# RWKV branch of an encoder layer: the group norm in three parts tied behind chunks, value shifts and loads tied behind later work, the norm's squares on VectorE

## The chip, the cores and the metric

The kernel runs on one core of a Trainium2 chip. The metric is device microseconds of one execution, the median of several runs on the same chip. Before the change it was 2368.71 us (three runs: 2364.8, 2368.71 and 2369.3).

Engine names in the rows: PE is TensorE (PEld its weight loads), DVE VectorE, ACT ScalarE, POOL GpSimd, SP SyncE. SP and POOL here mostly issue DMAs; each issues its own in the order of its instructions.

## The reference

One layer on 256 tokens of width 2048 in float32: a feed-forward block, two mixers in parallel (latent attention and RWKV-7) joined by gates, a cross-attention, a second feed-forward block. The change lies in the RWKV mixer:

```python
def rwkv7_branch(proj, mu_shift, w0, w_w2, a0, w_a2, w_g2, k_k, k_a, r_k, lnx_w, lnx_b, w_ob):
    p = token_shift(proj, mu_shift)              # y + (y_prev - y) * mu
    r, k, v, dw, da, dg = jnp.split(p, [...], axis=-1)
    g = jax.nn.sigmoid(dg) @ w_g2
    ...
    def step(state, inp):
        r_t, w_t, k_t, v_t, a_t, b_t = inp
        sa = jnp.einsum('bhvk,bhk->bhv', state, a_t)
        state = (state * w_t[:, :, None, :] + sa[..., None] * b_t[:, :, None, :]
                 + v_t[..., None] * k_t[:, :, None, :])
        return state, jnp.einsum('bhvk,bhk->bhv', state, r_t)
    _, o = lax.scan(step, s0, xs)                # 256 steps, 16 heads of 64
    ...
    mean = jnp.mean(o, axis=-1, keepdims=True)   # group norm, per head
    var = jnp.mean(jnp.square(o - mean), axis=-1, keepdims=True)
    o = ((o - mean) * lax.rsqrt(var + LNX_EPS)).reshape(B, S, C)
    o = o * lnx_w.astype(jnp.float32) + lnx_b.astype(jnp.float32)
    bonus = jnp.sum(rh * kh * r_k.astype(jnp.float32), axis=-1, keepdims=True) * vh
    return (((o + bonus.reshape(B, S, C)).astype(proj.dtype)) * g) @ w_ob
```

## The kernel before, in words

**The weight stream.** Every large product multiplies by weights that stream from memory. `weights` (line 192) loads tiles of 128x1024 floats on the SP queue (L203, four buffers `wraw`), and splits each into two parts that TensorE can take: ScalarE writes the high part `whi` (L205), VectorE the rest `wlo` (L206). The split tiles stand in a ring of three. One tile feeds 12 matmuls of 512 columns where the block is 512 wide (`lin_tok_steps`, L254 to L256: hi, lo, hi for each of two row halves), and a slot is freed when its last matmul is done. So each tile needs one turn of ScalarE and one of VectorE, and whatever else stands in these two queues delays the splits: an engine takes its instructions strictly in their written order.

**The mixer.** `mix` (line 1071) runs in stages. `rw_proj_v` (L715) projects the values in two blocks of 512 columns. Each half of a block is written to memory (`vraw`, L733), read back one row later (`vp`, L734), combined with a factor on VectorE (L735 to L737) and stored as `vsh` (L738). Then come the latent attention and, in one weave, the recurrent part together with a stream of plain products (`fill`: output products and eight gate blocks). `weave` writes TensorE's order by hand: a generator of recurrent steps yields how many microseconds of fill work should follow it.

**The recurrent part.** `rw_prep` (L748) makes decay, keys and receptances for each of two head groups; it loads two small weights `ww` on POOL (L754, L755), which the lora matmuls (L765) read. `rw_inverse` (L885) inverts small triangular blocks on VectorE, writes them to memory (`td`) and reads them back into `G` (L913). `rw_chain` (L926) then takes the 256 tokens in 8 chunks of 32. A chunk is: `po` + state (L954), `rhs` copy, `pu` (L964), `uv` copied half by ScalarE and half by VectorE (L967), `pn` (L973), the new state `S` on VectorE (L980, L981), `po` (L983), the next chunk's `po` (L939), `o` copied out (L991) and stored to `osc` on POOL (L993). Between those steps stand 9 to 12 matmuls of a gate block. `pn` waits for both halves of `uv`, so VectorE's copy is in the loop.

**Scale and norm.** For each half `t` of 128 tokens (four chunks) and each half `h` of the heads, `rw_scale` (L1000) loads `lnx_w`, `lnx_b` and the shifted values on POOL and prepares two factors `ab` (L1011 to L1017, with one matmul `pg` each, L1015). `rw_group_norm` (L1021) loads `ov` from `osc` on POOL and normalises: sum `gm` (L1029, L1030), subtraction (L1031), square on ScalarE (L1032), sum `gv` (L1033, L1034), the power -1/2 on POOL (L1035), and three products and sums (L1036 to L1038). The result is transposed (L334) into `z` for the last product. In `mix` the pieces for `t` = 0 are written as soon as two, four and six chunks have been stored, those for `t` = 1 behind the last chunk. They get a low priority, and a scheduler that plans with its own costs sets where each falls in an engine's queue. `after(a, b)` forces an order: a plain order if both are on one engine, a wait otherwise.

Of the kernel before, what the change touches and what calls it, by code (L numbers as in the profile page):

```python
# [10 lines left out]
F32 = mybir.dt.float32  # L11
F32R = mybir.dt.float32r
I32 = mybir.dt.int32
AF = mybir.ActivationFunctionType
# [4 lines left out]
P = 128  # L19
# [61 lines left out]
class Layer:  # L81
# [492 lines left out]
    def mla_heads(self, pool):  # L574
# [6 lines left out]
        for c in range(4):  # L581
# [132 lines left out]

    def rw_proj_v(self, mp, pool, normed):  # L715
        h, r, _ = normed
        nc = self.nc
        self.vraw = self.dram.tile([T + 1, 1024], F32, name="vraw")
# [5 lines left out]
        for c in range(2):  # L724
# [4 lines left out]
            def ev(t, ps):  # L729
# [19 lines left out]
    def rw_prep(self, pool, g, bon, ready):  # L749
# [5 lines left out]
        nc.gpsimd.dma_start(out=ww[64:], in_=a["w_a2"][:, cs])  # L755
# [243 lines left out]
    def rw_scale(self, pool, t, h, bon, behind):  # L999

        nc, a = self.nc, self.a
# [8 lines left out]
        v = ab[:, 1, :].rearrange("p (h v) -> p h v", v=64)  # L1010
        scaled = nc.vector.tensor_mul(v, v, bon[:, t, h * H : (h + 1) * H].unsqueeze(2).broadcast_to([P, H, 64]))  # L1011
        self.after(scaled, self.last_S)
        nc.vector.tensor_add(ab[:, 1, :], ab[:, 1, :], rows[:, 1, :])
        pg = self.psm.tile([P, 512], F32, tag="mm", name="pg")
        nc.tensor.matmul(pg, self.sg[:, ts], self.wg2[:, cs], start=True, stop=True)  # L1015
        self.after(nc.vector.tensor_mul(ab[:, 0, :], rows[:, 0, :], pg), self.last_S)
        nc.vector.tensor_mul(ab[:, 1, :], ab[:, 1, :], pg)  # L1017
        return ab

    def rw_group_norm(self, pool, t, h, ab):  # L1020
        nc = self.nc  # L1021
        H = HEADS_G
        ov = pool.tile([P, 2, 512], F32, tag="p4", name="ov", bufs=6)
        nc.gpsimd.dma_start(out=ov[:, 0, :], in_=self.osc[t * P : (t + 1) * P, h * 512 : (h + 1) * 512])
        o, sq = (ov[:, j, :].rearrange("p (h v) -> p h v", v=64) for j in range(2))
        bc = lambda x: x.unsqueeze(2).broadcast_to([P, H, 64])
        mean = self.stat.tile([P, H], F32, tag="gm", name="gm")
        var = self.stat.tile([P, H], F32, tag="gv", name="gv")
        nc.vector.tensor_reduce(out=mean, in_=o, axis=AX.X, op=ALU.add)  # L1029
        nc.vector.tensor_scalar_mul(mean, mean, 1.0 / 64)  # L1030
        nc.vector.tensor_sub(o, o, bc(mean))  # L1031
        nc.scalar.activation(out=sq, in_=o, func=AF.Square)  # L1032
        nc.vector.tensor_reduce(out=var, in_=sq, axis=AX.X, op=ALU.add)  # L1033
        nc.vector.tensor_scalar(out=var, in0=var, scalar1=1.0 / 64, scalar2=LNX_EPS, op0=ALU.mult, op1=ALU.add)  # L1034
        nc.gpsimd.tensor_tensor(out=var, in0=var, in1=self.mhalf.broadcast_to([P, H]), op=ALU.pow)  # L1035
        nc.vector.tensor_mul(o, o, bc(var))  # L1036
        nc.vector.tensor_mul(ov[:, 0, :], ov[:, 0, :], ab[:, 0, :])
        nc.vector.tensor_add(ov[:, 0, :], ov[:, 0, :], ab[:, 1, :])  # L1038
# [342 lines left out]
```

## Time and profile before

| | us |
|---|---|
| median of three runs | 2368.71 |
| lowest, highest | 2364.8, 2369.3 |
| the profiled execution, its own time | 2374.34 |
| its span, first to last instruction | 2372.2 |
| TensorE busy in the span | 2326.5 |
| mean granted TensorE clock, share of full | 0.991 |

TensorE is busy 98% of the span, so what can be gained without less work is in the 46 us in which it stood still, and in the stretches in which its clock was granted at half (1.2 instead of 2.4 GHz). Both are found stretch by stretch: a list of what TensorE waited for, and the granted clock by windows.

### The profile page before, as it was taken

Reading aid. Unit: us, or ns where it says so; the run is one execution under the profiler, and the core shown is the slowest. Engines: PE = TensorE matmul, PEld = TensorE weight load, DVE = VectorE, ACT = ScalarE, POOL = GpSimd, SP = SyncE. Lnnn points to the kernel's source line nnn. Section 1 sums busy time; section 2 is a strip of 40 time slices with the busy share of each in tenths; the row PEclk is TensorE's granted clock in tenths of the full one; section 3 lists DMA queues with packets and bytes.
Section 4 is the critical chain, followed back from the end, with each engine's and each line's share of the span. In section 5 each row is a group of like instructions: output and inputs, shape, how many; then the busy total and the mean of one; then the engine's idle time right before and its main releaser. Section 6 shows DMA issues by size and latency. Waiting matters only on the chain.

```text
span 2372.2 us, 34910 instructions
## 1 busy us (share of the span) xinstructions
PE 2326.5 (98%) x13610; PEld 1987.4 (84%) x13610; DVE 1453.2 (61%) x2117; ACT 1142.4 (48%) x1687; POOL 77.9 (3%) x128
## 2 busy tenths in 40 slices
PE   8999999999999999999999999999999999999997
PEld 7888888888887888888777788887888888888886
DVE  5666666654446576768556756656666666664444
ACT  6444544544446565534334546545544444444443
POOL 0000000000000100000122000000000000000000
PEclk9999999999999999999999999999999999999999
DMA  7555555566665664445647766545555555566664
GB/s 254 191 188 193 188 192 190 188 203 196 199 198 189 199 203 149 162 147 180 193 152 228 265 198 219 169 153 165 190 188 191 190 188 192 188 200 197 197 193 145
DMA packets 138821, 451.35 MB, mean 190 GB/s; under 512 B 24224, under 2 KB 26656, under 8 KB 138400
## 3 DMA queue, kind: packets, MB, share of 16 engines
q1 hardware_dynamic: 132992, 434.17, 56.4%
q0 software_dynamic: 4944, 14.69, 1.9%
q8 instruction: 106, 1.74, 0.3%
q10 hardware_dynamic: 720, 0.27, 0.1%
q14 instruction: 59, 0.48, 0.1%
HBM read 438.58 MB, written 10.49 MB: 189 GB/s over the span
## 4 chain that ended last, share of the span: by engine, by line
PE 49%; DVE 4%; DMA 2%; issue 1%; POOL 1%; ACT 0%; SPq 0%; DVEq 0%; POOLq 0%; ACTq 0%
PE mm L227 16%; PE mm L230 8%; PE mm L254 7%; PE mm L255 7%; PE mm L256 7%; DVE wlo L206 1%; DVE TT L908 0%; POOL gv L1035 0%; PE gr L870 0%; DVE X L436 0%; PE tr L361 0%; PE bt L874 0%; DVE tm L905 0%; PE xo L1260 0%; PE xsc L1249 0%
## 5 line engine op out<-in xcount | busy, mean ns | idle before, releaser
L206 DVE TENSOR_TENSOR wlo<-wraw,whi 128x1024 fp32r<-128x1024 f32 (+2 forms) x796 | 959.4, 1207 | 735.8 <-ACT whi L205 723.5
L205 ACT CAST whi<-wraw 128x1024 fp32r<-128x1024 f32 (+2 forms) x796 | 825.3, 1037 | 887.1 <-PE mm L256 453.5
L227 PE MATMUL mm<-hT,whi 128*128 128x512 f32 x3296 | 1149.5, 395 | 6.2 <-DVE hT L325 5.5
L230 PE MATMUL mm<-hT,wlo 128*128 128x256 f32 x3296 | 913.4, 283 | 2.0 <-DVE wlo L206 1.9
L227 PEld LDWEIGHTS mm<-hT,whi 128*128 128x128 f32 x3296 | 614.8, 189 | 134.8 <-ACT whi L205 6.3
L230 PEld LDWEIGHTS mm<-hT,wlo 128*128 128x128 f32 x3296 | 621.8, 189 | 12.5 <-DVE wlo L206 3.7
L254 PE MATMUL mm<-whi,mh 128*128 128x512 f32 x688 | 267.6, 389 | 0.0
L256 PE MATMUL mm<-whi,ml 128*128 128x512 f32 x688 | 267.6, 389 | 0.0
L255 PE MATMUL mm<-wlo,mh 128*128 128x512 f32 x688 | 267.6, 389 | 0.0
L255 PE MATMUL mm<-wlo,hT 128*128 128x512 f32 (+2 forms) x512 | 186.2, 364 | 6.7 <-DVE wlo L206 6.6
L254 PE MATMUL mm<-whi,hT 128*128 128x512 f32 (+2 forms) x512 | 190.4, 372 | 0.1
L256 PE MATMUL mm<-whi,hT 128*128 128x512 f32 (+2 forms) x512 | 185.0, 362 | 0.0
L254 PEld LDWEIGHTS mm<-whi,mh 128*128 128x128 f32 x688 | 129.1, 188 | 27.0
L256 PEld LDWEIGHTS mm<-whi,ml 128*128 128x128 f32 x688 | 129.1, 188 | 26.9
L255 PEld LDWEIGHTS mm<-wlo,mh 128*128 128x128 f32 x688 | 129.1, 188 | 26.6
L236 ACT COPY half<-mm 128x256 f32<-128x256 f32 x206 | 75.4, 367 | 135.2 <-PE mm L227 135.2
L237 DVE TENSOR_TENSOR half<-half,mm 128x256 f32<-128x256 f32 x206 | 86.0, 418 | 53.9 <-ACT half L236 53.9
L255 PEld LDWEIGHTS mm<-wlo,hT 128*128 128x128 f32 x512 | 97.5, 191 | 23.0 <-DVE wlo L206 9.8
L254 PEld LDWEIGHTS mm<-whi,hT 128*128 128x128 f32 x512 | 97.5, 190 | 16.4 <-ACT hT L324 0.5
L256 PEld LDWEIGHTS mm<-whi,hT 128*128 128x128 f32 x512 | 97.3, 190 | 14.4
L289 POOL TENSOR_TENSOR rstd<-rstd,mhalf 128x1 f32<-128x1 f32 x22 | 13.0, 597 | 1808.6 <-DVE rstd L287 1808.6
L254 PE MATMUL mm<-whi,oT 128*128 128x512 f32 x128 | 50.7, 396 | 0.0
(278 smaller groups left out, 1737.8 us busy)
## 6 DMA issues: line engine op xcount, KB each, us to landing
wraw<-in_w_ffn_up SPq DMA_DIRECT2D x172, 512.0 KB, 3.6
wraw<-in_w_ffn_gate SPq DMA_DIRECT2D x171, 512.0 KB, 4.2
wraw<-in_w_ffn_down SPq DMA_DIRECT2D x168, 512.0 KB, 4.2
wraw<-in_w_in SPq DMA_DIRECT2D x124, 512.0 KB, 3.5
wraw<-in_w_o SPq DMA_DIRECT2D x32, 512.0 KB, 3.5
wraw<-in_w_ckv SPq DMA_DIRECT2D x31, 512.0 KB, 3.5
wraw<-in_w_oa SPq DMA_DIRECT2D x16, 512.0 KB, 3.5
wraw<-in_w_ob SPq DMA_DIRECT2D x16, 512.0 KB, 4.3
```

Source lines behind the costliest of these rows:

```text
L205: cast = nc.scalar.copy(out=hi[:, e], in_=raw[:, e])
L206: self.last_split = nc.vector.tensor_sub(out=lo[:, e], in0=raw[:, e], in1=hi[:, e].bitcast(F32))
L227: both = lambda: nc.tensor.matmul(ps[j], hi[:, s], x[:, k], start=(k == 0), stop=(k == nk - 1))
L230: nc.tensor.matmul(ps[j][:, 0, :], lo[:, s], x[:, k, 0], start=False, stop=False)
L236: nc.scalar.copy(out=y, in_=ps[j][:, 1, :])
L237: nc.vector.tensor_add(y, y, ps[j][:, 0, :])
L254: nc.tensor.matmul(ps[t], part(xh, t, k), hi, start=(k == 0), stop=False)
L255: nc.tensor.matmul(ps[t], part(xh, t, k), lo, start=False, stop=False)
L256: self.last_mm = nc.tensor.matmul(ps[t], part(xl, t, k), hi, start=False, stop=(k == nk - 1))
L289: nc.gpsimd.tensor_tensor(out=r, in0=r, in1=self.mhalf, op=ALU.pow)
```

## The change

1. Value shift: the four VectorE instructions and the store of each half (L735 to L738) are put into a list, and written later: those of the first block in the middle of the second block's loop, those of the second block in `mla_heads`. The first instruction is tied behind the last split written by then.
2. The loads of `uv` for the first three chunks are tied behind the small `ww` loads.
3. `w_g2` and the `lnx`, `ab` loads of `t` = 0 were tied behind the write of the inverse; now they follow the store of the first chunk. Those of `t` = 1 follow the store of the seventh chunk (before, of the sixth). The arithmetic of `rw_scale` is separated: for `t` = 0 behind the third chunk, for `t` = 1 behind the last one.
4. The group norm takes both halves `h` together and has three parts: loads; sums up to the power; products. For `t` = 0 they are written behind the fourth, fifth and sixth chunk and tied behind that chunk's state update; the transposes follow the seventh. For `t` = 1 they are written behind the chain with 10 and 7 us of fill between, tied behind the last split.
5. The square is a VectorE product instead of a ScalarE activation.

```diff
+            if c == 1:
+                self.do_later()
...
-                nc.vector.tensor_sub(prev, prev, cur)
-                nc.vector.tensor_mul(prev, prev, mu)
-                nc.vector.tensor_add(prev, prev, cur)
-                nc.gpsimd.dma_start(out=self.vsh[t * P : (t + 1) * P, s], in_=prev)
-
-            self.lin_tok(self.a["w_in"], KD, 2880 + c * 512, 512, h[:, :, 0], h[:, :, 1], ev)
+
+                def shift(t=t, s=s, mu=mu):
+                    self.after(nc.vector.tensor_sub(prev, prev, cur), self.last_split)
+                    nc.vector.tensor_mul(prev, prev, mu)
+                    nc.vector.tensor_add(prev, prev, cur)
+                    nc.gpsimd.dma_start(out=self.vsh[t * P : (t + 1) * P, s], in_=prev)
+
+                self.later.append(shift)
+
+            for k in self.lin_tok_steps(self.a["w_in"], KD, 2880 + c * 512, 512, h[:, :, 0], h[:, :, 1], ev):
+                if k == 8:
+                    self.do_later()
...
-        nc.gpsimd.dma_start(out=ww[64:], in_=a["w_a2"][:, cs])
+        self.small = nc.gpsimd.dma_start(out=ww[64:], in_=a["w_a2"][:, cs])
...
-            self.nc.gpsimd.dma_start(
+            load = self.nc.gpsimd.dma_start(
                 out=uv[64 * h + 32 : 64 * h + 64].rearrange("s p v -> s (p v)"),
                 in_=self.vsh[c * CHUNK : (c + 1) * CHUNK, h * 512 : (h + 1) * 512])
+            if c < 3:
+                self.after(load, self.small)
...
+        ovs = []
+        for h in range(2):
+            ov = pool.tile([P, 2, 512], F32, tag="p4", name="ov", bufs=6)
+            nc.gpsimd.dma_start(out=ov[:, 0, :], in_=self.osc[t * P : (t + 1) * P, h * 512 : (h + 1) * 512])
+            ovs.append(ov)
...
-        nc.scalar.activation(out=sq, in_=o, func=AF.Square)
...
+        yield
+        behind = self.last_S if t == 0 else self.last_split
+        var = []
+        for ov in ovs:
...
+            self.after(nc.vector.tensor_reduce(out=mean, in_=o, axis=AX.X, op=ALU.add), behind)
+            nc.vector.tensor_scalar_mul(mean, mean, 1.0 / 64)
+            nc.vector.tensor_sub(o, o, bc(mean))
+            nc.vector.tensor_mul(sq, o, o)
...
+        yield
+        behind = self.last_S if t == 0 else self.last_split
+        for h, ov in enumerate(ovs):
+            o = heads(ov, 0)
+            self.after(nc.vector.tensor_mul(o, o, bc(var[h])), behind)
...
-                        if len(self.last_o) == 2 and (0, 0) not in ab:
...
-                                ab[0, h] = low(self.rw_scale, pool, 0, h, bon, self.inverted)
...
+                        if n == 1:
+                            self.wg2 = pool.tile([P, 1024], F32, tag="p4", name="wg2", bufs=6)
+                            self.after(nc.gpsimd.dma_start(out=self.wg2, in_=a["w_g2"]), self.last_o[0])
+                        if n in (1, 7):
                             for h in range(2):
-                                ab[1, h] = low(self.rw_scale, pool, 1, h, bon, self.last_o[5])
+                                scale[n // 7, h] = self.rw_scale(pool, n // 7, h, bon, self.last_o[n - 1])
+                        if n == 3:
+                            for h in range(2):
+                                ab[0, h] = next(scale[0, h])
+                        if n == 4:
+                            norm[0] = self.rw_group_norm(pool, 0, ab)
+                        if n in (4, 5, 6):
+                            next(norm[0])
+                        if n == 7:
+                            z_tiles(mp, "r", "k")
...
+                    norm[1] = self.rw_group_norm(pool, 1, ab)
+                    next(norm[1])
                     for h in range(2):
-                        z[1, h] = self.rw_group_norm(pool, 1, h, ab[1, h])
+                        ab[1, h] = next(scale[1, h])
+                    yield 10.0
+                    next(norm[1])
+                    yield 7.0
+                    next(norm[1])
                     z_tiles(pool, "ar", "bk")
-                    yield 26.0
+                    yield 9.0
```

Where this moves instructions is shown at three places. First VectorE's queue around the copy of `uv` for the sixth chunk (`gm`, `gv`, `ov` are the group norm's tiles of `t` = 0, `wlo` a split). Before:

```order
L1033 TENSOR_REDUCE gv<-ov 128x8
L1031 TENSOR_TENSOR ov<-ov,gm 128x512
L1034 TENSOR_SCALAR gv<-gv 128x8
L206 TENSOR_TENSOR wlo<-wraw,whi 128x1024
L1036 TENSOR_TENSOR ov<-ov,gv 128x512
L1033 TENSOR_REDUCE gv<-ov 128x8
L1037 TENSOR_TENSOR ov<-ov,ab 128x512
L1034 TENSOR_SCALAR gv<-gv 128x8
L1038 TENSOR_TENSOR ov<-ov,ab 128x512
L1036 TENSOR_TENSOR ov<-ov,gv 128x512
L206 TENSOR_TENSOR wlo<-wraw,whi 128x1024
L967 COPY uv<-pu 32x512
```

Now:

```order
L996 TENSOR_TENSOR S<-S,pn 128x512
L997 TENSOR_TENSOR S<-S,wc 128x512
L1060 TENSOR_REDUCE gm<-ov 128x8 x2
L1061 TENSOR_SCALAR gm<-gm 128x8 x2
L1062 TENSOR_TENSOR ov<-ov,gm 128x512 x2
L206 TENSOR_TENSOR wlo<-wraw,whi 128x1024
L1063 TENSOR_TENSOR ov<-ov 128x512 x2
L1064 TENSOR_REDUCE gv<-ov 128x8 x2
L1065 TENSOR_SCALAR gv<-gv 128x8 x2
L206 TENSOR_TENSOR wlo<-wraw,whi 128x1024
L983 COPY uv<-pu 32x512
```

The products that need POOL's power (L1036, now L1072) stood ahead of the copy; now they stand behind the next chunk's state update, and the sums all follow this chunk's.

Second, POOL's queue at the start of the chain (`wg`, `lnx`, `ab` are the loads for the scale, `osc` the store of a chunk). Before:

```order
L1133 DMA wg_9185<-in_w_g 128x1024
L1007 DMA lnx<-in_lnx_w 128x512
L1007 DMA lnx<-in_lnx_b 128x512
L1009 DMA ab<-vsh 128x512
L1007 DMA lnx<-in_lnx_w 128x512
L1007 DMA lnx<-in_lnx_b 128x512
L1009 DMA ab<-vsh 128x512
L921 DMA uv<-vsh 32x512
L993 DMA osc<-o 32x512 x2
```

Now:

```order
L935 DMA uv<-vsh 32x512
L1009 DMA osc<-o 32x512 x2
L935 DMA uv<-vsh 32x512
L1179 DMA wg_9690<-in_w_g 128x1024
L1024 DMA lnx<-in_lnx_w 128x512
L1024 DMA lnx<-in_lnx_b 128x512
L1026 DMA ab<-vsh 128x512
L1024 DMA lnx<-in_lnx_w 128x512
L1024 DMA lnx<-in_lnx_b 128x512
L1026 DMA ab<-vsh 128x512
```

The seven loads went behind the first chunk's store.

Third, VectorE's queue from the last chunk's copy on. Before:

```order
L967 COPY uv<-pu 32x512
L1050 SCALAR_TENSOR_TENSOR gt<-mm,rstd,g 128x512 x2
L206 TENSOR_TENSOR wlo<-wraw,whi 128x1024 x3
L1029 TENSOR_REDUCE gm<-ov 128x8 x2
L1030 TENSOR_SCALAR gm<-gm 128x8 x2
L1031 TENSOR_TENSOR ov<-ov,gm 128x512
L206 TENSOR_TENSOR wlo<-wraw,whi 128x1024
```

Now:

```order
L1030 TENSOR_TENSOR ab<-ab,bon 128x512
L1033 TENSOR_TENSOR ab<-ab,lnx 128x512
L206 TENSOR_TENSOR wlo<-wraw,whi 128x1024
L983 COPY uv<-pu 32x512
L1030 TENSOR_TENSOR ab<-ab,bon 128x512
L1087 SCALAR_TENSOR_TENSOR gt<-mm,rstd,g 128x512 x2
L206 TENSOR_TENSOR wlo<-wraw,whi 128x1024
...
L206 TENSOR_TENSOR wlo<-wraw,whi 128x1024
L1060 TENSOR_REDUCE gm<-ov 128x8
L1061 TENSOR_SCALAR gm<-gm 128x8
L1060 TENSOR_REDUCE gm<-ov 128x8
L206 TENSOR_TENSOR wlo<-wraw,whi 128x1024
```

Two instructions on the scale's loads now stand ahead of the last copy of `uv`; five on `ab` stand where "..." is; and two splits instead of three stand between the gate block's `gt` pair and the first sum.

## Rows read from the trace of the kernel before

**Rows 1.** What TensorE waited for, three stretches of the trace (700 to 830, 830 to 1000, 1100 to 1300 us): engine, line and tile, what ended the wait; total us, times, longest.
```profile
PE mm L255 <- DVE wlo L206: 1.8, 2, 1.6
...
PE lora L765 <- PE mm L256: 0.9, 1, 0.9
PE lora L765 <- DMA ww<-in_w_a: 0.7, 1, 0.7
...
PE mm L255 <- DVE wlo L206: 3.6, 3, 1.4
PE pn L973 <- DVE uv L967: 3.2, 2, 2.8
PE po L939 <- issue: 2.0, 1, 2.0
```

**Rows 2.** Busy time by windows (start:end, length, PE, PEld, DVE, ACT, POOL busy with instruction counts; then the granted TensorE clock as a share of full, the DMA share, GB/s). The first two are the stretches behind two pauses of the chain, the other two hold shorter pauses.
```profile
1146.70:1152.90 6.20, 6.19 (x43) 4.75 (x45) 1.23 (x1) 1.05 (x1) 0.00 (x0) 0.50 0.88 322
1217.90:1224.30 6.40, 6.40 (x63) 5.73 (x60) 3.60 (x5) 1.76 (x3) 4.28 (x8) 0.50 0.64 168
...
820.00:830.00 10.00, 8.36 (x36) 6.26 (x35) 8.83 (x11) 3.16 (x3) 1.09 (x2) 1.00 0.57 158
1262.00:1282.00 20.00, 16.43 (x72) 12.63 (x71) 16.30 (x24) 10.02 (x12) 6.67 (x6) 1.00 0.56 174
```

**Rows 3.** VectorE in order of time around the first value shift (start, us, engine, line, operation, tiles; in brackets the idle time before and what ended it), and POOL's two loads of `vp` for it.
```profile
819.84 0.69 DVE L735 TENSOR_TENSOR vp<-vp,vc 128x512 f32<-128x512 f32 x1 [5.02 <-DMA vp<-vraw]
821.18 1.22 DVE L206 TENSOR_TENSOR wlo<-wraw,whi 128x1024 fp32r<-128x1024 f32 x1
...
814.89 0.55 POOL L734 DMA_DIRECT2D vp<-vraw  x1 [2.61 <-DMA vraw<-vc]
816.68 0.54 POOL L734 DMA_DIRECT2D vp<-vraw  x1 [1.24 <-DMA vraw<-vc]
```

**Rows 4.** POOL in order of time at the three pairs of `uv` loads, ahead of the two `ww` loads.
```profile
933.54 2.98 POOL L921 DMA_DIRECT2D uv<-vsh  x6 [85.16 <-DMA wraw<-in_w_oa]
```

**Rows 5.** TensorE in order of time in the first chunk, around its longest pause there.
```profile
1143.92 0.80 PE L939 MATMUL po<-uv,G 32*64 32x64 f32 x20
1146.71 0.91 PE L939 MATMUL po<-uv,G 32*64 32x64 f32 x12 [1.99 <-issue]
```

**Rows 6.** DMA issues with size and median us from issue to landing: first in the window 1125 to 1145 us, then in 1219 to 1240 us; then, over all four `ab` loads, the landing times; last, what the queue that fetches instructions moved between 1144 and 1145 us (packets, MB, share of the 16 DMA engines' time).
```profile
wraw<-in_w_in SPq DMA_DIRECT2D x6, 512.0 KB, 8.6
G<-td SPq DMA_DIRECT2D x8, 64.0 KB, 7.5
ab<-vsh POOLq DMA_DIRECT2D x2, 256.0 KB, 8.7
...
wraw<-in_w_in SPq DMA_DIRECT2D x3, 512.0 KB, 3.5
ab<-vsh POOLq DMA_DIRECT2D x2, 256.0 KB, 6.0
...
DMA to landing us min/median/max: 5.5/7.1/9.6
...
q8 instruction: 1, 0.02, 7.3%
```

**Rows 7.** VectorE in order of time from ahead of the fifth chunk's copy to the sixth's.
```profile
1198.88 0.69 DVE L1029 TENSOR_REDUCE gm<-ov 128x8 f32<-128x512 f32 x1 [2.22 <-DMA ov<-osc]
...
1204.03 0.69 DVE L1031 TENSOR_TENSOR ov<-ov,gm 128x512 f32<-128x512 f32 x1
1204.63 0.69 DVE L981 TENSOR_TENSOR S<-S,wc 128x512 f32<-128x512 f32 x1
...
1213.61 0.69 DVE L1036 TENSOR_TENSOR ov<-ov,gv 128x512 f32<-128x512 f32 x1 [1.53 <-POOL gv L1035]
...
1215.47 0.69 DVE L967 COPY uv<-pu 32x512 f32<-32x512 f32 x1
```

**Rows 8.** TensorE in order of time in the sixth chunk: all but the first two matmuls of `pn`.
```profile
1216.21 1.14 PE L973 MATMUL pn<-uv,bk 64*64 64x64 f32 x30 [2.79 <-DVE uv L967]
```

**Rows 9.** The store of the seventh chunk (POOL), the last chunk's copy (VectorE) and the matmuls that wait for it (TensorE), each from its engine's timeline.
```profile
1236.31 1.01 POOL L993 DMA_DIRECT2D osc<-o  x2 [12.26 <-ACT o L991]
...
1245.84 0.69 DVE L967 COPY uv<-pu 32x512 f32<-32x512 f32 x1
...
1247.37 1.08 PE L983 MATMUL po<-uv,G 32*32 32x64 f32 x32
```

**Rows 10.** VectorE behind the chain, around the sums and the first product of `t` = 1.
```profile
1257.18 0.69 DVE L1029 TENSOR_REDUCE gm<-ov 128x8 f32<-128x512 f32 x1 [0.65 <-DMA ov<-osc]
1261.26 0.69 DVE L1029 TENSOR_REDUCE gm<-ov 128x8 f32<-128x512 f32 x1 [3.39 <-DMA ov<-osc]
...
1264.99 0.17 DVE L1034 TENSOR_SCALAR gv<-gv 128x8 f32<-128x8 f32 x1
...
1267.85 0.69 DVE L1036 TENSOR_TENSOR ov<-ov,gv 128x512 f32<-128x512 f32 x1 [1.56 <-POOL gv L1035]
```

**Rows 11.** TensorE behind the chain, where the first pause for a split there ends; and, earlier, the `pg` pair of the second chunk with the matmul behind it.
```profile
1263.94 0.50 PE L255 MATMUL mm<-wlo,hT 128*128 128x512 f32 x1 [1.42 <-DVE wlo L206]
...
1162.71 1.98 PE L1015 MATMUL pg<-wg,sg 128*128 128x512 f32 x4
1164.13 0.80 PE L254 MATMUL mm<-whi,hT 128*128 128x512 f32 x1
```

More of the change, by code (lines that the diff above doesn't have):

```diff
@@ L713, in rw_proj_lora, with do_later @@
         self.lin_ch(self.a["w_in"], KD, 3904, 256, h, ev)
+    def do_later(self):
+        for f in self.later:
+            f()
+        self.later = []
     def rw_proj_v(self, mp, pool, normed):
@@ L717, in rw_proj_v @@
         nc = self.nc
+        self.later = []
         self.vraw = self.dram.tile([T + 1, 1024], F32, name="vraw")
@@ L1009, in rw_scale @@
         self.after(nc.gpsimd.dma_start(out=ab[:, 1, :], in_=self.vsh[ts, cs]), behind)
[L1010 to L1020, printed above, removed]
+        def arithmetic():
+            v = ab[:, 1, :].rearrange("p (h v) -> p h v", v=64)
+            scaled = nc.vector.tensor_mul(
+                v, v, bon[:, t, h * H : (h + 1) * H].unsqueeze(2).broadcast_to([P, H, 64]))
+            self.after(scaled, self.last_S)
+            nc.vector.tensor_add(ab[:, 1, :], ab[:, 1, :], rows[:, 1, :])
+            pg = self.psm.tile([P, 512], F32, tag="mm", name="pg")
+            nc.tensor.matmul(pg, self.sg[:, ts], self.wg2[:, cs], start=True, stop=True)
+            self.after(nc.vector.tensor_mul(ab[:, 0, :], rows[:, 0, :], pg), self.last_S)
+            nc.vector.tensor_mul(ab[:, 1, :], ab[:, 1, :], pg)
+            yield ab
@@ L1021, in rw_group_norm @@
+        return arithmetic()
+    def rw_group_norm(self, pool, t, ab):
         nc = self.nc
         H = HEADS_G
-        ov = pool.tile([P, 2, 512], F32, tag="p4", name="ov", bufs=6)
-        nc.gpsimd.dma_start(out=ov[:, 0, :], in_=self.osc[t * P : (t + 1) * P, h * 512 : (h + 1) * 512])
-        o, sq = (ov[:, j, :].rearrange("p (h v) -> p h v", v=64) for j in range(2))
-        bc = lambda x: x.unsqueeze(2).broadcast_to([P, H, 64])
-        mean = self.stat.tile([P, H], F32, tag="gm", name="gm")
@@ L1036, in rw_group_norm @@
[L1036 to L1039 removed]
+        ovs = []
[3 more added lines that the diff above has]
+            ovs.append(ov)
+        heads = lambda ov, j: ov[:, j, :].rearrange("p (h v) -> p h v", v=64)
@@ L1041, in gate_steps @@
+        yield
[3 more added lines that the diff above has]
+            self.after(nc.vector.tensor_mul(o, o, bc(var[h])), behind)
+            nc.vector.tensor_mul(ov[:, 0, :], ov[:, 0, :], ab[t, h][:, 0, :])
+            nc.vector.tensor_add(ov[:, 0, :], ov[:, 0, :], ab[t, h][:, 1, :])
+        self.normed = [ov[:, 0, :] for ov in ovs]
+        yield
     def gate_steps(self, pool, normed, c, use):
@@ L1129, in rwkv @@
                     self.rw_inverse(pool, G)
-                    keep = tc.cur_priority
-                    tc.cur_priority = E
-                    self.wg2 = pool.tile([P, 1024], F32, tag="p4", name="wg2", bufs=6)
-                    self.after(nc.gpsimd.dma_start(out=self.wg2, in_=a["w_g2"]), self.inverted)
-                    E2 = tc.cur_priority
-                    tc.cur_priority = keep
-                    ab, z = {}, {}
+                    E2, ab, scale, norm = E, {}, {}, {}
                     def low(f, *args):
@@ L1157, in rwkv @@
-                        if len(self.last_o) == 7 and (1, 0) not in ab:
-                            for h in range(2):
-                                ab[1, h] = low(self.rw_scale, pool, 1, h, bon, self.last_o[5])
+                                ab[0, h] = next(scale[0, h])
[5 more added lines that the diff above has]
+                            z_tiles(mp, "r", "k")
+                            for h in range(2):
+                                self.transposed(self.normed[h], zh, zl, None, 0, 4 * h)
@@ L1160, in rwkv @@
+                    seen = 0
+                    for want in self.rw_chain(pool, G):
+                        if len(self.last_o) > seen:
+                            seen = len(self.last_o)
+                            low(behind_chunk, seen)
                         yield want
                     tc.cur_priority = E2
+                    norm[1] = self.rw_group_norm(pool, 1, ab)
+                    next(norm[1])
                     for h in range(2):
-                        z[1, h] = self.rw_group_norm(pool, 1, h, ab[1, h])
+                        ab[1, h] = next(scale[1, h])
```

25 lines of the change are left out of this document (9 added, 16 removed).

## Prediction

> **What bounds the kernel now.** I read the busy table first: TensorE works 2326.5 of the 2372.2 us, so any gain is a pause or a stretch at half clock. The list of TensorE's waits, taken stretch by stretch, shows which pauses the change can touch [rows 1]: 1.8 us at the first value shift, 1.6 us at the lora matmuls, and in and behind the chain 2.0 us in the middle of a group of `po` matmuls, 3.2 us at `pn`, 3.6 us for splits. Last the granted clock [rows 2]. Behind the 2.0 us pause and behind the long one at `pn` it is 0.50, the lower level of 1.2 GHz, for 6.2 and 6.4 us; around the pause at 820 us, the longest of its stretch with 1.6 us, and over the three pauses behind the chain, none over 1.4 us, it is 1.00. So in this trace a pause of 2 us or more is paid twice: the pause, and half of the slow stretch behind it, 3.1 or 3.2 us. I found no other engine that is the bound; VectorE matters only where its queue holds back a split or the copy of `uv`.
>
> The sum is made against the profiled execution, 2374.3 us (2.1 us of it outside the span), and taken off the median, 2368.7; the profiled one is 5.6 us longer, which I assume is the same before and after.
>
> **The change, part by part.**
>
> *(a) First value shift.* VectorE stood 5.0 us waiting for `vp` with a split, ready, behind it in the queue [rows 3]; TensorE ran out of splits. The new order puts one more split (1.2 us) ahead of the first subtraction and holds both subtractions ahead of the next. That covers the wait for the first tile. The second tile's load is issued 1.8 us later [rows 3] and, landing as late behind its issue as the first, holds the queue until some 1.8 us behind the first; so I expect two short pauses, 0.5 and 0.4 us, in place of 1.8: -0.9, with ends 0 and -1.8. The second block's shift keeps its place in VectorE's order, and its stores on POOL have nothing urgent behind them.
>
> *(b) Lora loads.* Six `uv` loads took POOL 3.0 us right ahead of the two `ww` loads [rows 4], and TensorE waited 1.6 us for these [rows 1]. With `ww` first they land 3 us earlier: -1.6. The `uv` loads, now behind the second `ww`, are not read for over 100 us. Ends: -0.8 and -1.6.
>
> *(c) Loads at the start of the chain.* The 2.0 us pause stands between the 20th and the 21st of 32 equal matmuls [rows 5], where no data can be missing; the profile names no releaser. The queue that fetches instructions moved one block in the microsecond in which the pause begins, and all transfers of that stretch were slow: 7.5 to 8.7 us to landing, against 3.5 and 6.0 later [rows 6]. I take it for an instruction block that was late behind the traffic. The seven loads on POOL (`w_g2`, four `lnx`, two `ab`) were part of that traffic; they now start behind the first chunk's store, that is behind the pause. If it goes, so does its slow stretch: 2.0 + 6.2/2 = -5.1. The other end is 0: the traffic of the write-back and the weight tiles is enough for it, or the seven loads meet the next block. I take -5.1, since two of the three streams in those rows remain, but the third, seven loads of 256 or 512 KB, goes.
>
> The Trainium skill (Runtime: NRT & Kernel Launch, "Instruction fetch mechanics") has the sequencer fetch blocks of 256 instructions through its own DMA queue while it works on the one before, "mostly hidden". By that rule the pause is something else and (c) is 0, the third case below. The trace agrees with the block (0.02 MB) but shows one pause that nothing else explains.
>
> *(d) Group norm of the first half.* VectorE's queue waited 2.2 us for `ov`, with the copy of `uv` behind it, and later 1.5 us for POOL's power, with a split and the next copy behind [rows 7]; `pn` came 0.4 us late in the fifth chunk, 2.8 us late in the sixth [rows 1, 8], and 6.4 us at half clock followed. In the new order no wait on POOL or on a load is ahead of these copies. What is: from the end of the fifth chunk's state update to the copy's end eight large operations at the pitch of 0.60 us that independent ones have [rows 7], two of them the new squares, four small ones at 0.1, two splits at 1.2, the copy at 0.7, in all 8.3 us. The update itself ends about 2 us earlier than its 1205.3 us [rows 7], without the late `pn` and the three group norm steps mixed into it, at 1203.3; so the copy ends at 1211.6, and `pn` wants it at 1213.4 - 0.4 = 1213.0. 1.4 us to spare. The third part (six operations, 3.6 us) has the same window for itself. So -0.4 - 2.8 - 3.2 = -6.4. The squares leave ScalarE (0.63 us each, no one waits there). Ends: -6.4 and -2.8, where a pause under 2 us is left at the sixth chunk.
>
> *(e) The last chunk's copy.* Ahead of it now stand two operations on the scale's loads. These are issued behind the seventh chunk's store, at 1236.3 us in the old clock [rows 9]: 1.0 us of stores, then `ab` as the third load, at +2.1. Landing took 6.0 us there, 9.6 at most [rows 6]. So the first operation starts at +8.1, and with the second, a split and the copy (0.6 + 0.7 + 1.2 + 0.7) the copy ends at +11.3; TensorE wants it at 1247.4, that is +11.1, or some 0.4 sooner because the transposes that moved here are shorter than the `pg` pair that left: a pause of 0.6 us. +0.6; ends 0 and +7.3 (landing 3.6 later, and the slow stretch of 3.1 that a pause of 4 us brings).
>
> *(f) Group norm of the second half.* Before, three splits stood between the gate block's `gt` and the first sum, and the second sum waited until 1261.3 us for its load [rows 10], 13.9 us behind the last chunk's `po` at 1247.4 [rows 9]. Now two do, so the third split is behind that wait: 13.9 + 0.7 + 1.2 = 15.8. TensorE came to the fourth tile at 1263.9 - 1.4 = 1262.5 [rows 11], to the third one tile (12 matmuls, 2.7 us) sooner, +12.4; the `pg` pair, which now stands here, adds 1.4 [rows 11]: 13.8. A pause of 2.0. Then 0.4 at the next split. From the power's operand to its product it takes 2.9 us [rows 10], and now one reduction instead of a split lies between; with two more squares in the queue I get another pause of 2.4 us and one of 0.1. In all 4.9 for 3.6: +1.3. Two of these are of the size at which the clock fell in the chain; I count one slow stretch, +3.1. Together +4.4. Ends: -1.1 (the load lands 2 us sooner, no slow stretch) and +7.5 (two slow stretches).
>
> Sum: -0.9 - 1.6 - 5.1 - 6.4 + 0.6 + 4.4 = -9.0, so 2368.7 - 9.0 = 2359.7.
>
> **The rivals.**
>
> *No slow stretch behind the chain.* For it: full-width matmuls precede these pauses, small ones preceded the 2.0 us pause that cost the clock. 2359.7 - 3.1 = 2356.6.
>
> *The pause at the start stays.* For it: DMA is as busy there from `G` and four weight tiles. 2359.7 + 5.1 = 2364.8, within 0.2%. This is also what the page's rule would give.
>
> *Late loads in the last chunk.* Landing at 9.6 instead of 6.0 us makes the pause 4.2 us and costs the clock: 2359.7 + 3.6 + 3.1 = 2366.4. Against it: 9.6 was seen only in the full stretch at the start. The Trainium skill (DMA: Bandwidth & Descriptors, "Rules for kernel authors") says to issue a DMA early and wait for it late; this change does the opposite with these loads, and this case is what the rule gives here. The rows agree in so far as the old order, with the loads a chunk sooner, never waited.
>
> *VectorE runs out in the tied chunks: slower.* The parts are tied behind a state update with the next copy behind them. If they take over 1.4 us more than counted, `pn` waits again, now in three chunks (sixth, seventh, last) instead of one, each at the old price of 2.8 + 3.2 = 6.0 us: 2359.7 + 18.0 = 2377.7. Against it: the pitch of 0.60 is read from the same operations; the part behind the sixth chunk's update has six operations, where this one has twelve.
>
> **How the numbers follow.** Forecast 2359.7, rounded to 2360: 0.38. No slow stretch behind the chain, 2356.6: 0.22. Pause at the start stays, 2364.8: 0.17. Late loads, 2366.4: 0.14. VectorE runs out, 2377.7: 0.09. The bound of 0.2%, about what a measurement of this kernel can tell from no change, is 2364.0 and 2373.4. The first two cases are faster; the third lies at the bound, and I give 0.02 of it to faster: 0.62. Same: 0.15 + 0.14 = 0.29. Slower: 0.09. The range: its low end is the second case with (a) and the waits of (f) at their best, 2356.6 - 0.9 - 2.4 = 2353; its high end covers the fourth case with half of the remaining end of (f), 2369; beyond are the fifth case and some of the mixtures, under 0.2.
>
> **What would show it.** In the new trace: no wait of TensorE near the second value block over 0.6 us; none at lora; none in the `po` group of the first chunk, and a clock of 1.00 behind it; none at `pn` of the fifth and sixth chunk; a short one at the last `po`; and two pauses for splits of about 2 us behind the chain, with one stretch at 0.50. It would be wrong if the `pn` pauses stay, if the pause at the start turns up again one or two chunks later, or if the splits behind the chain wait much longer than 5 us.

## The result and the profile after

The changed kernel takes 2353.18 us (median of 4 runs, 2350.66 to 2355.01), the kernel before 2368.03 (2364.8 to 2369.3): a ratio of 0.9943, 95% interval 0.9925 to 0.9961, so 14.85 us less by the medians (13.5 by the ratio), where the prediction had 9.0 less. The profiled execution took 2350.66 us, its span is 2348.7.

What TensorE waited for in the three stretches of [rows 1], in the changed kernel (same columns; the middle stretch, at lora, has no wait left):

```profile
PE mm L255 <- DVE wlo L206: 0.4, 1, 0.4
...
PE mm L255 <- DVE wlo L206: 1.0, 1, 1.0
PE po L999 <- DVE uv L983: 0.4, 1, 0.4
```

The first row was 1.8 us at the first value shift. The 1.6 us at lora are gone. Of the 8.8 us in and behind the chain 1.4 are left: no wait at `pn`, none without a releaser ("issue", a pause for which the profile shows no reason) in the `po` group of the first chunk. The waits of [rows 1] fall from 12.2 to 1.8 us.

Busy time by windows (columns as in [rows 2]; the granted clock is the third number from the end): the start of the chain, the sixth chunk, the stretch behind the chain.

```profile
1130.00:1150.00 20.00, 19.95 (x320) 16.05 (x320) 10.47 (x12) 7.88 (x12) 5.79 (x11) 1.00 0.88 266
1198.00:1212.00 14.00, 14.00 (x197) 11.27 (x196) 9.45 (x13) 4.17 (x6) 3.41 (x4) 1.00 0.33 103
1240.00:1260.00 20.00, 18.95 (x85) 14.94 (x84) 18.09 (x25) 8.21 (x9) 5.95 (x6) 1.00 0.63 208
```

The clock is 1.00, the upper level of 2.4 GHz, in all three. The two slow stretches of [rows 2] are gone with their pauses, and the one that the prediction had behind the chain did not come.

VectorE in order of time, at the places of [rows 3, 7 and 10] (start, us, line, tiles; idle time before): the first value shift; the sums of the first half, with the products two chunks' work later; the last chunk; the second half behind the chain.

```profile
816.34 1.51 DVE L745 TENSOR_TENSOR vp<-vp,vc 128x512 f32<-128x512 f32 x2 [1.44 <-DMA vp<-vraw]
...
1189.87 1.27 DVE L1060 TENSOR_REDUCE gm<-ov 128x8 f32<-128x512 f32 x2
...
1198.66 0.69 DVE L983 COPY uv<-pu 32x512 f32<-32x512 f32 x1
...
1203.90 1.29 DVE L1072 TENSOR_TENSOR ov<-ov,gv 128x512 f32<-128x512 f32 x2
...
1223.91 0.69 DVE L1030 TENSOR_TENSOR ab<-ab,bon 128x512 f32<-128x512 f32 x1 [3.00 <-DMA ab<-vsh]
...
1226.50 0.69 DVE L983 COPY uv<-pu 32x512 f32<-32x512 f32 x1
...
1238.41 0.69 DVE L1060 TENSOR_REDUCE gm<-ov 128x8 f32<-128x512 f32 x1 [3.05 <-DMA ov<-osc]
1239.22 0.68 DVE L1060 TENSOR_REDUCE gm<-ov 128x8 f32<-128x512 f32 x1
...
1248.28 0.69 DVE L1072 TENSOR_TENSOR ov<-ov,gv 128x512 f32<-128x512 f32 x1 [1.20 <-POOL gv L1067]
```

Sums and products of the first half (no brackets) wait for nothing, and each stands behind a state update, where the next copy of `uv` is not due yet. The last chunk's copy stands behind a 3.0 us wait for `ab`; TensorE pays 0.4 of it (the row at `po` above). Behind the chain the second load of `ov` landed with the first.

### The profile page after: what moved, and what is told of

Its sections match the earlier page's. It is cut to its first block, busy times and chain, and to the rows that moved or that the text cites. A ratio compares the mean times of both kernels' runs of the same rounds, so it can differ in the third digit from the quotient of the medians.

```text
span 2348.7 us, 34905 instructions
## 1 busy us (share of the span) xinstructions
PE 2314.8 (99%) x13610; PEld 1980.3 (84%) x13610; DVE 1454.9 (62%) x2121; ACT 1138.5 (48%) x1683; POOL 76.0 (3%) x128
## 4 chain that ended last, share of the span: by engine, by line
PE 91%; issue 3%; DVE 3%; DMA 2%; ACT 1%; POOL 0%; SPq 0%; DVEq 0%; POOLq 0%; ACTq 0%
PE mm L227 30%; PE mm L230 16%; PE mm L254 13%; PE mm L255 13%; PE mm L256 13%; DVE wlo L206 1%; DVE X L436 1%; PE gr L884 0%; PE po L955 0%; PE tr L361 0%; PE po L999 0%; PE tr L334 0%; PE pn L989 0%; PE bt L888 0%; PE pu L980 0%
```

## The experiments

Twelve kernels, in three groups, each group on one chip with runs of the kernel before beside it. Ratios are to those runs ("by the ratio": the difference of two ratios times the time of the kernel before); for the changed kernel the ratio is 0.9943, and 0.9938 (0.9923 to 0.9953) when it was run again.

**loads_early** undoes (c).

```
-  self.after(nc.gpsimd.dma_start(out=self.wg2, in_=a["w_g2"]), self.last_o[0])
+  self.after(nc.gpsimd.dma_start(out=self.wg2, in_=a["w_g2"]), self.inverted)
-  scale[n // 7, h] = self.rw_scale(..., self.last_o[n - 1])
+  scale[n // 7, h] = self.rw_scale(..., self.last_o[n - 1] if n == 7 else self.inverted)
```

> The changed kernel with its third part undone: the seven loads for the scale (w_g2, four lnx, two ab) are issued behind the write-back of the inverse again, ahead of the first chunk, and nothing else moves on any engine. Theory (late instruction block: traffic at the start of the chain delays the block that TensorE's sequencer is to run next): a pause near 2.0 us is back between the 20th and the 21st matmul of the first po group, no releaser named, half clock for some 6 us behind it; +5.1 us on 2353.2, near 2358. Rival (chance: the pause comes in some runs, whatever these loads do): no pause, 2353.

Measured: 2355.07 us, ratio 0.9946 (0.9931 to 0.9960): 0.7 to 1.9 us more than the two ratios of the changed kernel, inside the intervals. In its trace, TensorE in order of time:

```profile
1135.99 0.79 PE L955 MATMUL po<-uv,G 32*64 32x64 f32 x19
1137.62 0.62 PE L955 MATMUL po<-uv,G 32*64 32x64 f32 x13 [0.84 <-issue]
```

A pause without a releaser is back in the same group, one matmul record from where [rows 5] has it, but of 0.84 us. The granted clock over the 24 us from 1128 on is 0.92 and 0.94, 1.7 us lost.

**before_loads_late** does (c) alone in the kernel before (the same two conditions).

> The kernel before with the third part alone: the seven loads start behind the first chunk's store. Theory: no pause in the first po group and clock 1.00 behind it, the pauses at pn of the fifth and sixth chunk as before, 2368.0 - 5.1 = 2363 us, unless pg or the scale, two chunks in here and not three, now waits for the loads. Rival (chance): the pause stays, 2368.

Measured: 2365.0 us, ratio 0.9993 (0.9981 to 1.0005). No pause in the first `po` group, clock 1.00 there; at `pn` one pause of 2.6 us and half clock behind, as in [rows 8]. The trace says what was expected, but for the 0.4 us at `pn` of the fifth chunk, which is gone too; the time gained is 1.7 us by the ratio, 2.3 by the medians, not 5.1.

**dummy_traffic** adds seven transfers into a scratch area behind the write-back.

```
+  junk = self.dram.tile([P, 4096], F32, name="junk")
+  self.after(nc.gpsimd.dma_start(out=junk[:, :1024], in_=a["w_g2"]), self.inverted)
+  for j in range(6):
+      self.after(nc.gpsimd.dma_start(out=junk[:, 1024 + j * 512 : 1536 + j * 512], in_=src), self.inverted)
```

> The changed kernel, its loads where it has them, and seven more transfers of the same sizes and sources (2 MB) that nobody reads, issued behind the write-back of the inverse into a scratch area in device memory. Theory (traffic alone delays the instruction block): the pause near 2.0 us is back in the first po group, with half clock behind, near 2358. Rival (it was not the traffic but the buffers that these loads fill, or their place in POOL's queue): no pause, 2353.

Measured: 2364.36 us, ratio 0.9986 (0.9976 to 0.9997), some 10 us more than the changed kernel. TensorE's waits between 1120 and 1265 us:

```profile
PE pu L980 <- ACT rhs L974: 5.8, 1, 5.8
PE mm L255 <- DVE wlo L206: 1.0, 1, 1.0
PE pn L989 <- DVE uv L983: 0.7, 1, 0.7
PE po L955 <- issue: 0.4, 1, 0.4
PE po L999 <- DVE uv L983: 0.3, 1, 0.3
```

The pause without a releaser is back (0.4), at the same matmul as in loads_early. Most of the price came another way: the `G` loads took 11.0 us to landing, and ScalarE stood 11.0 us before a cast of a weight tile, whose load is issued behind these on SP, with the copy of `rhs` behind it in its queue. So traffic nobody reads is enough to make the start of the chain late; the buffers are not needed for it. It is a harder case than the seven loads, though: the `G` loads took 7.1 us in loads_early.

**four_more_matmuls, early_4_more, early_2_more** were to move the ends of TensorE's instruction blocks (the blocks that the instruction queue of [rows 6] moves): four (or two) lora matmuls are issued twice, in the kernel before and in loads_early.

```
+  for _ in range(2 if (g, p2) == (0, 0) else 1):
       nc.tensor.matmul(pl[x][:, j, :], ww[q, p * P : (p + 1) * P], self.twa[q], start=True, stop=True)
```

> The kernel before with four lora matmuls of the first group issued twice, some 240 us ahead of the chain; the result of the second is that of the first. Each is as many TensorE instructions as one po matmul: two passes with a weight load each. Theory (the pause stands where one block of TensorE's instructions ends): it moves eight passes ahead in the po group, to between the 12th and the 13th. Rival (it is bound to a time or to a datum of the chain): it stays between the 20th and the 21st.

> The kernel of loads_early with four lora matmuls of the first group issued twice (same result), each as many TensorE instructions as one po matmul, that is two passes with their weight loads. In loads_early, in dummy_traffic and in the kernel before the pause stood behind 51 or 52 passes of the two po groups of the first chunk (19 or 20 of the second 32). Theory (end of an instruction block): if a pause without a releaser comes, it stands eight passes sooner, behind the 11th or 12th of the second 32. Rival (a time or a datum): behind the 19th or 20th, as before.

> The kernel of loads_early with two lora matmuls issued twice. Theory (end of an instruction block): a pause without a releaser, if it comes, stands four passes sooner, behind the 15th or 16th of the second 32 passes of po. Rival (a time or a datum): behind the 19th or 20th.

Measured: 2364.12, 2355.34 and 2359.62 us, one run each. No pause without a releaser in any of the three; TensorE stood still earlier, at `pu`, for the `G` loads. Their rows, in this order:

```profile
1140.36 1.05 PE L965 MATMUL pu<-rhs,G 32*32 32x64 f32 x30 [1.68 <-DMA G<-td]
```
```profile
1134.63 1.23 PE L981 MATMUL pu<-rhs,G 32*32 32x64 f32 x30 [2.00 <-DMA G<-td]
```
```profile
1135.41 1.88 PE L981 MATMUL pu<-rhs,G 32*32 32x64 f32 x30 [3.69 <-DMA G<-td]
```

So these three could not tell a block's end from a time; when the blocks came, which does, is told under (c) below. They showed something else: with the seven loads early, the first chunk is late in every trace, but not always at the same place. And in four_more_matmuls, which has the old group norm, `pn` of the sixth chunk waits 0.7 us only, with the clock at 1.00:

```profile
1212.53 1.14 PE L974 MATMUL pn<-uv,bk 64*64 64x64 f32 x30 [0.71 <-DVE uv L968]
```

**norm_whole** undoes (d): for the first half sums, squares (on ScalarE), power and products stand together, untied, behind the fourth chunk.

```
   if n == 4:
-      norm[0] = self.rw_group_norm(pool, 0, ab)
-  if n in (4, 5, 6):
-      next(norm[0])
+      self.normed = [self.old_norm(pool, 0, h, ab[0, h]) for h in range(2)]
```

> The changed kernel with its fourth part undone for the first half: sums, squares (on ScalarE again), power and products of the group norm stand together behind the fourth chunk, tied to nothing, as before; loads, scale and transposes stay where the change has them. Theory (VectorE's queue waited for the ov load and for POOL's power with the copy of uv behind): pauses at pn near 0.4 us in the fifth and 2.8 us in the sixth chunk are back and half clock behind the longer one, +6.4 on 2353.2, near 2360 us. Rival (the late pn of before came of the chain's start, 2 us late by the pause there): no pause at pn over 0.7 us, clock 1.00, 2353 to 2354.

Measured: 2360.09 us, ratio 0.9968 (0.9956 to 0.9980), 5.9 us more than the changed kernel by the ratio, 6.9 by the medians. TensorE, and behind it VectorE, in order of time in the sixth chunk:

```profile
1207.53 1.14 PE L989 MATMUL pn<-uv,bk 64*64 64x64 f32 x30 [2.81 <-DVE uv L983]
```
```profile
1204.93 0.69 DVE L1094 TENSOR_TENSOR ov<-ov,gv 128x512 f32<-128x512 f32 x1 [1.53 <-POOL gv L1093]
1205.54 1.22 DVE L206 TENSOR_TENSOR wlo<-wraw,whi 128x1024 fp32r<-128x1024 f32 x1
1206.79 0.69 DVE L983 COPY uv<-pu 32x512 f32<-32x512 f32 x1
```

The 2.81 us at `pn` stand where [rows 8] had 2.79: the product waits 1.53 us for POOL's power, the split and the copy wait behind it. The clock is 0.87 and 0.85 in the two windows of 12 us from 1200 on, 3.4 us lost. The start of the chain had no pause here, so the rival is out. The 0.4 us of the fifth chunk did not come back.

**squares_on_scalar** puts the four squares back on ScalarE, ties kept.

```
-  nc.vector.tensor_mul(sq, o, o)
+  nc.scalar.activation(out=sq, in_=o, func=AF.Square)
```

> The changed kernel with the four squares on ScalarE as before, all ties kept. Theory (the ties and the three parts do it, not the engine of the squares): no pause at pn over 0.5 us, clock 1.00, within 1.5 us of 2353.2. Rival (with the round trip to ScalarE in VectorE's queue, ahead of the copy of uv, the 1.4 us that the prediction found to spare are gone): a pause at pn of the sixth chunk of 1 to 2 us, with half clock behind 2 us, up to +4, 2357.

Measured: 2355.13 us, ratio 0.9953 (0.9939 to 0.9967). No wait at `pn`: the rival is out. But the median is 1.9 us above 2353.2, where the theory allowed 1.5, and the pause at the power's product behind the chain is 2.1 us, not 1.0, since both powers now come together (4.32 us for the two); the theory did not have that.

**tail_old** undoes (f): behind the chain the parts are neither split nor tied, the squares are on ScalarE, and the scale stands in the last chunk.

```
-  norm[1] = self.rw_group_norm(pool, 1, ab)
...
-  yield 10.0
-  next(norm[1])
-  yield 7.0
-  next(norm[1])
+  self.normed = [self.old_norm(pool, 1, h, ab[1, h]) for h in range(2)]
```

> The changed kernel with its sixth part undone: behind the chain the group norm of the second half is not split nor tied, its squares are on ScalarE, and its scale stands in the last chunk as before. Theory read from the trace of after (the parts, tied behind splits, keep VectorE's queue free of waits for the load and the power): TensorE waits for splits 3.6 us in all behind the chain again, against 1.0, so +2.6 on 2353.2, near 2356 us. Rival (the order matters little; the tail was cheap since both loads of ov were issued together and landed early): TensorE waits about 1 us, 2353.

Measured: 2354.27 us, ratio 0.9945 (0.9933 to 0.9957), 0.5 to 1.7 us more. Two pauses, 1.8 and 0.8 us, 2.6 in all (3.6 was expected) against 1.0, and a clock of 0.86 over 12 us, 1.7 lost. In the trace the new order is the better one; in time the difference lies inside the intervals.

**shift_lora_old** undoes (a) and (b).

```
-  self.after(nc.vector.tensor_sub(prev, prev, cur), self.last_split)
+  nc.vector.tensor_sub(prev, prev, cur)
...
-  self.later.append(shift)
+  shift()
...
-  if c < 3:
-      self.after(load, self.small)
```

> The changed kernel with its first two parts undone: the value shifts stand where their block's copy is, and the uv loads go ahead of the ww loads on POOL. Theory: TensorE waits about 1.8 us near the second value block and 1.6 us at lora again, +3.0 on 2353.2, near 2356 us. Rival (the waits move with the time at which the loads land, not with this order): under 1 us in all, 2353 to 2354.

Measured: 2357.5 us, ratio 0.9961 (0.9948 to 0.9973), 4.3 us more. TensorE's waits between 700 and 1000 us:

```profile
PE mm L255 <- DVE wlo L206: 2.1, 2, 1.7
PE lora L779 <- DMA ww<-in_w_a: 1.0, 1, 1.0
PE lora L779 <- PE mm L256: 0.6, 1, 0.6
```

Both waits are back near their old sizes, 3.3 us more than in the changed kernel. Another 1.4 is a split behind the chain, which has nothing to do with (a) and (b): there the second `ov` load landed later.

**changed_again** is the changed kernel, with no edit.

> The changed kernel once more, for more times of it and a second trace. Theory: median 2352 to 2355 us; no pause in the first po group nor at pn; a pause of about 1.0 us at the power's product behind the chain, with 0 to 1.5 at the split before it. Rival (the profiled run of the changed kernel was a lucky one): a pause over 1 us between 1130 and 1225 us.

Measured: 2351.56 us (2348.05 to 2355.39), ratio 0.9938 (0.9923 to 0.9953). In the chain the list names no wait, behind it one:

```profile
1250.30 0.50 PE L255 MATMUL mm<-wlo,hT 128*128 128x512 f32 x1 [0.99 <-DVE wlo L206]
```

**loads_and_parts_moved** takes away the 1.4 us that are left: `ab` a chunk sooner, the sums one split later, the products behind two splits.

```
-  if n in (1, 7):
+  if n in (1, 6):
...
-  yield 10.0
+  yield 12.5
...
-  yield 7.0
+  yield 9.7
...
-  yield 9.0
+  yield 6.3
```

> The changed kernel with two small moves: the scale's loads of the second half are issued a chunk sooner (behind the sixth chunk's store), and behind the chain the sums of the group norm stand one split later and its products behind two splits, not one, after the power. Theory from the runs so far (the pause at the last po is the wait for ab; the first split pause behind the chain is how far the second ov load lands behind 12.2 us after the last po; the second, 0.98 to 1.02 us in every run, is the power's time): the pause of 0.4 at the last po is gone, the first split pause too, and the second is 0 to 0.3 us; 1.4 to 2.5 us less than the changed kernel on the same chip. Rival (what is late moves on: the transposes of z or the products now come late for the output matmuls): a pause of 1 us or more near the next transposes, and no gain.

Measured: 2349.23 us (2346.82 to 2353.42), ratio 0.9932 (0.9916 to 0.9948), 2.3 us under the changed kernel on the same chip by the medians, 1.4 by the ratios. TensorE waits for nothing between 1120 and 1290 us. VectorE there:

```profile
1239.61 0.69 DVE L1060 TENSOR_REDUCE gm<-ov 128x8 f32<-128x512 f32 x1 [1.65 <-DMA ov<-osc]
...
1250.43 0.69 DVE L1072 TENSOR_TENSOR ov<-ov,gv 128x512 f32<-128x512 f32 x1 [0.92 <-POOL gv L1067]
```

VectorE's waits for the load and for the power are still there, but no split that TensorE wants stands behind them. The trace bears the theory out; in time the two intervals overlap, so the gain is not shown.

## Why the prediction was right, and where its sum was off

The measured 2353.18 us lie 6.5 below the forecast and only 0.2 above the low end of the stated range, 2353, which its own working puts at 2353.3 (and the high end at 2366.4 + 3.1/2 = 2368.0, not 2369): that it fell inside is luck. The sum is off mainly by (f), 7.0 us better in the trace than predicted; (c), which by time was worth less than predicted, made up some of that. The assumption that the profiled execution is 5.6 us longer than the median, before and after, did not hold: after, it is 2.5 shorter.

*(a)* -0.9 predicted; 0.4 of 1.8 us is left, so -1.4. The order did what was said. The second `vp` tile did not land 1.8 us behind the first: both subtractions run in one go at 816.34. shift_lora_old brings the wait back.

*(b)* -1.6, as predicted; shift_lora_old brings 1.6 back.

*(c)* -5.1 predicted. That the early loads make the first chunk late is shown: six traces with them, or with dummy traffic in their place, have a pause there (2.0, 1.7, 0.8, 2.0, 3.7 and 5.8 + 0.4 us, in [rows 5] and the experiments as told), each with half clock near it; eight traces without them have none at all. `G` took 7.5 us to landing in [rows 6]; over 1110 to 1160 us of the changed kernel it is 2.5:

```profile
G<-td SPq DMA_DIRECT2D x8, 64.0 KB, 2.5
```

The size was taken from one trace. The five traces with the real loads lose 2.5 to 7.2 us there, pause and slow stretch together; the timed runs differ by 0.7 to 2.3 us only. Why timed runs pay less than traces stays open. The rival "the pause at the start stays" is out for this kernel.

The step "an instruction block that was late" is borne out by the times at which the blocks came. In every trace the queue q8 moved 106 blocks of 16 KB, one for about 257 of the 27,299 to 27,316 recorded instructions of TensorE. The block next to the pause, in loads_early from 1135 to 1136 us, in dummy_traffic from 1134 to 1135, in the changed kernel from 1131 to 1132 (columns as at the end of [rows 6]):

```profile
q8 instruction: 1, 0.02, 6.4%
...
q8 instruction: 1, 0.02, 7.4%
...
q8 instruction: 1, 0.02, 7.0%
```

In the kernel before, loads_early and dummy_traffic it began at 1144.24, 1135.09 and 1134.13 us, 5.1 to 6.9 us after TensorE had passed the place 256 instructions ahead of the pause, and took 1.0 to 1.2 us. The pause ended 1.3, 1.5 and 1.3 us after it was in, each time behind 12,993 or 12,994 recorded instructions. In the eight traces without early loads it began 0.9 to 1.5 us after that place and was in 4.0 to 4.8 us before TensorE needed it. In the three kernels that were to move the pause it was in over 12 us before, so they could not show one. Counted in steps of 256 from the pause, none of the other places in the 14 traces, over 1,400, had its block in less than 1.6 us ahead. No run delayed a block and nothing else; the three pauses agree in time and place. The Trainium skill (Runtime: NRT & Kernel Launch, "Instruction fetch mechanics") calls the fetch mostly hidden. By that sentence alone (c) would have been 0; the traces agree with it at all these places but three, and in those three 2 MB of other transfers were in flight.

*(d)* -6.4 predicted, and the term that time bears out best: norm_whole gives it back with the same 2.8 us at `pn`, 3.4 us (3.2 in the prediction) of lost clock, and 5.9 to 6.9 us of time. The size still moves from trace to trace: the four with the old order wait 2.8, 2.6, 2.8 and 0.7 us at the sixth chunk (the kernel before, before_loads_late, norm_whole, four_more_matmuls). In the last one the load of `ov` held VectorE up for 0.2 us, not 2.2, and the clock did not fall. The 0.4 us of the fifth chunk stood in the kernel before alone. The rival "VectorE runs out" did not come: the second part begins at 1189.87, and with two splits among its operations the copy behind it starts 8.8 us later, at 1198.66, without a wait of TensorE, whose `pn` comes at 1200.13:

```profile
1200.13 1.15 PE L989 MATMUL pn<-uv,bk 64*64 64x64 f32 x32
```

From the end of the state update to the copy's end it was 9.4 us, not 8.3: the sum left out that the splits wait for ScalarE, 0.75 and 0.29 us here. The copy ended 0.8 us ahead of `pn`, where the sum had 1.4. Behind the third part, too, the copy comes without a wait of TensorE. That the squares moved to VectorE made no difference in the chain (squares_on_scalar).

*(e)* +0.6 predicted, +0.4 measured, 0.2 to 0.6 in the other traces of this order where the list names a wait; in three it names none, but the last `po` group takes 1.4 to 1.5 us there, not 1.1. The rival "late loads" (+3.6 and a slow stretch) never came. The Trainium skill (DMA: Bandwidth & Descriptors, "Rules for kernel authors") says to issue a DMA early. Here the trace agrees (a chunk sooner, the 0.4 is gone); at the start of the chain it does not, where the same kind of load, issued early, held back what was needed first.

*(f)* is the step that failed: +4.4 predicted, -2.6 measured (1.0 for 3.6 us), and no slow stretch. The mechanism was right, its sizes were not:
- The first pause was put at 2.0 us, with the second sum as late behind the last `po` as before. In the nine traces of the new order the sum starts 10.8 to 12.6 us behind the end of that `po`, and TensorE pays what goes over 11.2: 12.6 gives 1.44 (shift_lora_old), 12.3 gives 1.07 (early_2_more), 12.0 gives 0.81 (norm_whole), 11.1 and less give 0. In the changed kernel it was 10.9 (1239.22 less 1227.24 and 1.08). Had the load landed as in [rows 10], 12.8, the pause would have been 1.6.
- The second was put at 2.4 us; it is 0.98 to 1.02 in all but one trace of this order, 2.1 where the squares are on ScalarE. The power took 1.67 us where it had taken 2.57, and the product waited 1.20 us for it, not 1.56 as in [rows 10].
- One slow stretch of 3.1 us was counted, for pauses of 2 us; the rival without it (0.22) came true in this point. In the changed kernel no pause was that long; where one was, 2.1 us in squares_on_scalar, the clock stayed at 1.00, and in tail_old one of 1.8 us cost 1.7.

With what the runs showed, (a), (b), (d), (e) and (f) make -1.4 - 1.6 - 6.4 + 0.4 - 2.6 = -11.6, and (c) between -0.7 and -5.1: -12.3 to -16.7. Measured: -14.85, and -14.7 by the ratio when it was run again. The profiled pair differs by 23.7 us (2374.34 to 2350.66); most of the rest is half clock elsewhere, which comes and goes from run to run (below).

## What to carry to other kernels

An operation on an in-order engine that waits for a load, or for another engine, is charged to whatever critical copy stands behind it: tie it to the place right behind such a copy, and split it where it waits. Move loads that are not urgent out of the stretch in which a write-back must be read again, but not so late that their reader stands ahead of a critical copy. Before a single trace's pause is put into a sum at its full size, look at a second trace: here the pause at the start was 0.8 to 3.7 us in the kernels with the early loads, and the one at `pn` 0.7 to 2.8 us in those with the old norm.

## What the hardware did that was not expected

The same pause costs the clock in one run and not in another. All traces have a 2.6 us wait of TensorE near 728 us, which the change does not touch. Busy time from 720 to 744 us, in the kernel before, in tail_old and in the changed kernel:

```profile
720.00:744.00 24.00, 21.00 (x90) 16.69 (x88) 16.59 (x31) 14.03 (x30) 1.63 (x3) 0.86 0.69 210
```
```profile
720.00:744.00 24.00, 20.75 (x99) 16.41 (x98) 17.98 (x34) 15.95 (x35) 1.63 (x3) 0.93 0.75 231
```
```profile
720.00:744.00 24.00, 20.56 (x104) 16.39 (x103) 19.07 (x37) 16.26 (x36) 1.63 (x3) 1.00 0.77 218
```

A clock of 0.86, 0.93 or 1.00 over 24 us is 3.4, 1.7 or 0 us lost behind the same wait. What decides between them no run here shows. It is part of the spread of the kernel before, 2358.4 to 2371.7 us in 23 runs on one chip, which goes with the mean clock in the main: the two fastest have 0.996, the two with 0.991 took 2369.3 and 2370.1 (the slowest, 2371.7, has 0.993).

POOL's power of 128x8 values takes longer when it starts while VectorE runs a split than when it starts while VectorE runs a reduction. From its operand to its product, VectorE in tail_old and in the changed kernel:

```profile
1248.16 1.22 DVE L206 TENSOR_TENSOR wlo<-wraw,whi 128x1024 fp32r<-128x1024 f32 x1
1250.94 0.69 DVE L1094 TENSOR_TENSOR ov<-ov,gv 128x512 f32<-128x512 f32 x1 [1.56 <-POOL gv L1093]
```
```profile
1246.41 0.67 DVE L1064 TENSOR_REDUCE gv<-ov 128x8 f32<-128x512 f32 x1
```

The power is 2.57 us long in the first and 1.67 in the second, and it starts within 0.2 us of the row shown first. What counts is what runs at its start: the first power of `t` = 0 in the changed kernel starts at 1197.07 us, 0.33 us ahead of a split, and takes 1.66. Over all 14 traces a power that starts inside a two-input operation of VectorE is longer the more is left of that operation: 2.5 to 2.7 us with 1.0 to 1.2 us left, 2.0 to 2.1 with 0.5 to 0.6, 1.8 with 0.3; all others take 1.6 to 1.7.
